# Products of the output projections in the order 2, 1, 4, 6, 5, 7, 3, rows fetched group by group, and the later modulations in other stages

## The chip, the cores and the metric

The kernel runs on one core of a Trainium2 chip. The metric is the device time of one execution in microseconds (us); lower is better. The core has TensorE (PE, matrix products into PSUM banks), VectorE (DVE), ScalarE (ACT) and GpSimd (POOL), and issues transfers (DMAs) from the queues of SyncE (SP) and POOL. Each engine takes its instructions in the order in which they stand in its program.

## The reference, cut to what matters

One layer over 1024 latent tokens and 256 context tokens of width 1024, all in float32. `ml` and `mc` hold nine modulation vectors each, from `silu(c) @ w_mod + b_mod`.

```python
x  = x  + 0.5*ml[2]*swiglu(modulate(rms_norm(x,  g1), ml[0], ml[1]), ffn1_w_in, ffn1_w_out)
cx = cx + 0.5*mc[2]*swiglu(modulate(rms_norm(cx, g1), mc[0], mc[1]), ffn1_w_in, ffn1_w_out)
# mixers on modulate(rms_norm(x, g2), ml[3], ml[4]): gated convolution and attention
x  = x + ml[5]*merge(...)
x  = x + 0.5*ml[8]*swiglu(modulate(rms_norm(x, g3), ml[6], ml[7]), ffn2_w_in, ffn2_w_out)
out = rms_norm(x, final_g)
# swiglu(h, w_in, w_out): a, b = split(h @ w_in); (silu(a)*b) @ w_out, with an inner width of 2816
```

## The kernel before, in words

Activations lie transposed: 128 channels on the partitions, tokens in two chunks C0 and C1 of 512. A float32 product is made of three products of halves: ACT casts an operand to its high part (`rh`, `wh`, ...), DVE subtracts that for the low part (`rl`, `wl`, ...), and PE multiplies high by high, high by low, low by high. Every instruction goes through one helper, so that all rows of the profile name line 88.

The stages follow each other: first modulations and norm; FFN1-in (to about 720 us), 22 columns of the inner width, j = 0 to 21 (L1094); FFN1-out (735 to 956); eight mixers with their weights from `w_in` (956 to 1350, L1191); projections, attention and merge (to about 2100); FFN2-in (to about 2508); FFN2-out with the final norm.

Each FFN-out is `row_products` (L773). It multiplies a 2 x 2 block matrix of weights, A11 to A22, with the 2 x 2 blocks B11 to B22 of the hidden rows in seven products in place of eight (a Winograd scheme). Product i runs over 11 rows of 128, taken in six groups k = 0, 2, 4, 6, 8, 10 (the last has one row), with 12 matmuls a row: 132 matmuls. Products 1, 6 and 7 add up in one set of four PSUM banks, `chain` (names `pt`, `pt`, `po`, `ps`); the others take four of five `ps` banks. At a product's end its banks are added to `x` by DVE (`add`, out of `to`, L859), and only then may a product that uses those banks go on. The order of products stands in L864. `operands` (L815) gives the two operands of a row: the left one from weights (`raw`, or `ws`, where A-sums are made by accumulating DMAs of POOL's queue), the right one from the row tiles (`hid`), which DVE turns into sums in place after their use. The row tiles are written by FFN1-in to DRAM (`hd`) and fetched by `Rows.fetch` (L766), all at once, quadrant after quadrant. In FFN2-out product 3 is made in two halves of 256 tokens: all its split operands are kept (`kept`), so that the second half goes output by output, beside the final norm of the chunks that are done (`final`, L1594).

`after1(i, k)` and `after3(i, k)` (L1144, L1642) are called behind each group and put work in between: loads and stores of the residual `x`, squares for the next norm (`square`), steps of the mixers' first norm (`norm0`, L501: sum of squares of C0, its inverse root `rstd_cols`, a broadcast of that by PE, eight multiplications, splits into the operands `r1` and `r2`).

A later modulation (`later_mod`, L262) is a generator: for each half vector eight loads of `w_mod` (`rawm`), each followed by a multiply-add into `macc` on DVE, then a cast `acch` on ACT with its low part, two matmuls, and four small transfers that turn the row into columns (`mcol`, `modl`): 19 steps a half. FFN1-in runs STEPS[j] steps behind column j (L1100, up to 15), mixers i > 1 run 11 each (L1197), and what is left runs behind the mixers (L1216).

The order on each engine is made at build time by a list scheduler with a model of times; it keeps data dependences and the program order of what is marked (`pinned`, and what is issued while `strict` is set).

Of the kernel before, what the change touches and what calls it, by code (L numbers as in the profile page):

```python
# [18 lines left out]
P = 128  # L19
D = 1024  # L20
# [21 lines left out]
STEPS = (0, 6, 6, 6, 7, 7, 8, 8, 8, 15)  # L42
# [7 lines left out]
def tile_dit_layer(  # L50
# [413 lines left out]
    class Winograd:  # L464
# [6 lines left out]
        def __init__(self, xs, gain, mod, m, pairs, plain=False, ahead=3, side_from=None):  # L471
# [10 lines left out]
            self.n_squares = 0  # L482
# [18 lines left out]
        def norm0(self, in_place=False):  # L501

            acc = sum_squares(self.xs, C0)
            yield
            y = rstd_cols([acc], 512, D)
# [10 lines left out]
        def square(self, d):  # L516

            if not self.n_squares:
                self.acc = [ttile("sq_acc")]
            sq = ttile("sq") if self.n_squares else self.acc[0]  # L520
            act.activation(out=sq, in_=self.xs(d, C1), func=AF.Square)
            if self.n_squares == KD - 1:
                self.acc.append(sq)
            elif self.n_squares:
                dve.tensor_add(out=self.acc[0], in0=self.acc[0], in1=sq)
            self.n_squares += 1

        def norm1(self):
            y = rstd_cols(self.acc, 512, D)
# [215 lines left out]
    class Rows:  # L745


        def __init__(self, n, name):

            self.n, self.t = n, {}  # L750
# [15 lines left out]
        def fetch(self, src):  # L766

            for lower, c in ((0, 0), (0, 1), (1, 0), (1, 1)):
                for k, m in self.groups:
                    j = lower * self.n + k  # L770
                    load(self.t[k, lower, c], src[j : j + m, :, c * 512 : (c + 1) * 512].rearrange("a p n -> p a n"))

    def row_products(w, rows, add, after=lambda i, k: None, halves=False):  # L773
# [9 lines left out]

        R, groups = P * rows.n, rows.groups
        sums = {}
# [12 lines left out]

        def minus(t):
            act.activation(out=t, in_=t, func=AF.Copy, scale=-1.0)  # L800
# [13 lines left out]

        def operands(i, k, m):  # L815
# [174 lines left out]
    half1.acc = accs  # L990
# [39 lines left out]
    def all_later_mods():  # L1030
# [5 lines left out]
        for m in range(2, 9):  # L1036
            yield from later_mod(m)

    steps = all_later_mods()


# [68 lines left out]

    gate1 = half_gate("gate1", 2)
# [22 lines left out]
    hs = Rows(NH // 2, "hid")  # L1134
    hs.fetch(hd)
# [570 lines left out]
```

## Time and profile before

| | |
|---|---|
| median of 3 runs | 2775.6 us (2775.3 to 2777.56) |
| profiled execution | 2770.1 us |
| its span in the trace | 2768.2 us |
| mean granted clock of PE | 0.981 |
| PE busy | 2668.4 us (96%) |
| DVE busy | 2012.0 us (73%) |
| ACT busy | 1153.5 us (42%) |
| DMA, mean | 128 GB/s |

The profile is of one execution. A group row reads: line, engine, operation, output <- inputs, shape, count | total busy, mean ns | idle time before it and what ended it. A waits row reads: engine and output of the one that waited <- what it waited for: us in all, times, the longest. Times in the timeline are counted from the span's start.

### The profile page before, as it was taken

The numbers are of one execution on the slowest core, as the hardware profiler recorded it, in microseconds if no ns is written. First come the engines' busy times: TensorE is split into PE (matmuls) and PEld (weight loads), VectorE is DVE, ScalarE is ACT, GpSimd is POOL, SyncE is SP. The second block draws the span as 40 slices with busy tenths as digits, with TensorE's granted clock in tenths as the row PEclk, the third lists the DMA queues.
The fourth block names the chain that finished last, engine by engine and source line by source line (L and its number), as shares of the span: only waits on it lengthen the run. The fifth ranks groups of instructions, "written<-read, shape, count | busy, mean of one in ns | idle before, by whom it ended". The sixth has DMA issues, their size and how long they took to land.

```text
span 2768.2 us, 37334 instructions
## 1 busy us (share of the span) xinstructions
PE 2668.4 (96%) x13625; PEld 2248.5 (81%) x13625; DVE 2012.0 (73%) x3356; ACT 1153.5 (42%) x2293; POOL 543.0 (20%) x419
## 2 busy tenths in 40 slices
PE   7898999999799999999999999999999999999989
PEld 4687988888677777788899888887888788888878
DVE  5887688887787789887568676685548776568874
ACT  4524333333244552333344566574226333334542
POOL 2240122221011014333123211100000442330110
PEclk8899999999899999999999999999999999999999
DMA  8265433444965244434312311001444542228641
GB/s 308 92 203 159 137 122 122 135 131 150 369 188 112 92 152 151 157 99 134 107 47 63 117 62 61 24 32 41 150 125 129 168 130 76 85 91 292 147 98 62
DMA packets 355649, 354.37 MB, mean 128 GB/s; under 512 B 27382, under 2 KB 248712, under 8 KB 355464
## 3 DMA queue, kind: packets, MB, share of 16 engines
q1 hardware_dynamic: 346440, 334.68, 36.7%
q0 software_dynamic: 9024, 17.30, 4.0%
q8 instruction: 107, 1.75, 0.3%
q14 instruction: 78, 0.64, 0.1%
HBM read 287.91 MB, written 63.96 MB: 127 GB/s over the span
## 4 chain that ended last, share of the span: by engine, by line
PE 80%; DVE 10%; DMA 4%; issue 3%; ACT 2%; POOL 1%; SPq 1%; DVEq 0%; ACTq 0%; POOLq 0%
PE ps L88 66%; PE po L88 7%; PE pt L88 7%; DMA raw<-in_ffn_w_out_dram 2%; DVE wl L88 1%; DVE r L88 1%; DVE macc L88 1%; DMA rawm<-in_w_mod_dram 1%; DVE nt L88 1%; SPq L88 1%; DVE x L88 0%; DMA mcol<-mrow 0%; DVE hid L88 0%; DVE u L88 0%; DVE wo L88 0%
## 5 line engine op out<-in xcount | busy, mean ns | idle before, releaser
L88 PE MATMUL ps<-r,wl 128*128 128x512 f32 x5280 | 1234.2, 393 | 25.4 <-ACT r L88 9.8
L88 PEld LDWEIGHTS ps<-r,wl 128*128 128x128 f32 x5280 | 992.5, 189 | 242.3 <-ACT r L88 12.4
L88 ACT CAST wl<-s 128x512 fp32r<-128x512 f32 x256 | 158.3, 620 | 361.8 <-PE ps L88 270.6
L88 ACT CAST wl<-raw 128x512 fp32r<-128x512 f32 x278 | 172.0, 620 | 283.7 <-PE ps L88 173.5
L88 POOL TENSOR_TENSOR s<-raw 128x512 f32<-128x512 f32 x64 | 97.3, 1521 | 976.3 <-DMA raw<-in_ffn_w_in_dram 553.5
L88 DVE TENSOR_TENSOR wl<-raw,wl 128x512 fp32r<-128x512 f32 x276 | 196.6, 713 | 85.5 <-ACT wl L88 84.2
L88 DVE TENSOR_TENSOR wl<-s,wl 128x512 fp32r<-128x512 f32 x256 | 223.9, 876 | 13.4 <-ACT wl L88 11.7
L88 POOL TENSOR_TENSOR s<-raw,s 128x512 f32<-128x512 f32 x64 | 101.0, 1579 | 404.7 <-DVE wl L88 404.7
L88 DVE SCALAR_TENSOR_TENSOR macc<-rawm,silu_c,macc 128x512 f32<-128x512 f32 x168 | 146.6, 891 | 16.7 <-DMA rawm<-in_w_mod_dram 15.7
L88 PE MATMUL ps<-wh,r 128*128 128x256 f32 x768 | 141.6, 285 | 0.0
L88 DVE TENSOR_TENSOR u<-u,ps 128x512 f32<-128x512 f32 x168 | 114.4, 681 | 34.9 <-PE ps L88 33.3
L88 DVE TENSOR_TENSOR pts<-pt,pts 128x512 fp32r<-128x512 f32 x160 | 108.7, 687 | 42.1 <-ACT pts L88 41.0
L88 ACT CAST rh<-hid 128x512 fp32r<-128x512 f32 x132 | 80.7, 620 | 135.7 <-PE ps L88 103.5
L88 DVE TENSOR_REDUCE m<-ps 128x1 f32<-128x512 f32 (+1 forms) x192 | 110.9, 596 | 28.7 <-PE ps L88 27.7
L88 PE MATMUL ps<-rh,wl 128*128 128x512 f32 x360 | 126.1, 393 | 3.5 <-DVE x L88 3.5
L88 ACT CAST pts<-pt 128x512 fp32r<-128x512 f32 x160 | 93.0, 592 | 86.6 <-PE pt L88 84.9
L88 PEld LDWEIGHTS ps<-wh,r 128*128 128x128 f32 x768 | 120.6, 192 | 0.0
L88 DVE TENSOR_TENSOR rl<-hid,rh 128x512 fp32r<-128x512 f32 x132 | 89.9, 687 | 31.1 <-PE ps L88 29.6
L88 PE MATMUL po<-pts,vh 128*128 128x512 f32 x256 | 110.3, 437 | 1.5 <-ACT pts L88 1.5
L88 PE MATMUL ps<-wl,r 128*128 128x256 f32 x384 | 108.8, 283 | 0.0
L88 ACT CAST wh<-raw 128x512 fp32r<-128x512 f32 (+1 forms) x84 | 67.1, 803 | 95.2 <-PE ps L88 80.2
L88 PE MATMUL ps<-kl,qs 128*128 128x512 f32 x384 | 106.0, 397 | 0.4 <-ACT pc L88 0.4
(280 smaller groups left out, 5098.6 us busy)
## 6 DMA issues: line engine op xcount, KB each, us to landing
raw<-in_ffn_w_in_dram SPq DMA_DIRECT2D x117, 512.0 KB, 4.5
raw<-in_ffn_w_out_dram SPq DMA_DIRECT2D x72, 512.0 KB, 5.7
rawm<-in_w_mod_dram SPq DMA_DIRECT2D x128, 256.0 KB, 4.3
raw<-in_w_in_dram SPq DMA_DIRECT2D x61, 512.0 KB, 3.7
hid<-hd SPq DMA_DIRECT2D x40, 512.0 KB, 9.4
ws<-in_ffn_w_out_dram POOLq DMA_DIRECT2D x30, 512.0 KB, 6.5
hd<-c SPq DMA_DIRECT2D x38, 256.0 KB, 2.0
hd<-u SPq DMA_DIRECT2D x38, 256.0 KB
```

What stands on the lines that cost most here:

```text
L88: inst = getattr(self.engine, name)(*args, **kw)
```

## The change

Products of both FFN-outs come in the order 2, 1, 4, 6, 5, 7, 3. Hidden rows are fetched in pieces, at the start the first two groups of B21, the rest from within products 2 and 1. Sums of rows and weights are made in another way (`sums`), in program order on their engines; s1 = A12 + A22 and s2 = A11 - s1 get buffers of their own. C0's squares for the mixers' norm are made as its rows are done, and the steps of that norm come at other places of products 7 and 3. FFN1-in runs only modulations up to 5; mods 6, 7 and 8 go into mixers i > 1 (13 steps each) and into FFN2-in (3 a column); `gate3` follows FFN2-in. The steps of the final norm come at other groups, and the last chunk's transposes ahead of its inverse root. Cut to its core:

```diff
-STEPS = (0, 6, 6, 6, 7, 7, 8, 8, 8, 15)
+STEPS = (0, 6, 6, 6, 7, 7, 8, 8, 8, 12)
...
-            yield
-            y = rstd_cols([acc], 512, D)
+            if C0 not in self.accs:
+                self.accs[C0] = [sum_squares(self.xs, C0)]
+                yield
+            y = rstd_cols(self.accs[C0], 512, D)
...
+        def square(self, d, ch=C1):
+
+            accs, n = self.accs.setdefault(ch, []), self.n_squares.get(ch, 0)
+            sq = ttile("sq" if n else "sq_acc")
+            act.activation(out=sq, in_=self.xs(d, ch), func=AF.Square)
+            if n in (0, KD - 1):
+                accs.append(sq)
+            else:
+                dve.tensor_add(out=accs[0], in0=accs[0], in1=sq)
+            self.n_squares[ch] = n + 1
 
         def norm1(self):
...
+        def fetch(self, lower, c, to):
+
+            for k, m in self.groups[:to]:
+                if (k, lower, c) not in self.fetched:
+                    self.fetched.add((k, lower, c))
                     j = lower * self.n + k
-                    load(self.t[k, lower, c], src[j : j + m, :, c * 512 : (c + 1) * 512].rearrange("a p n -> p a n"))
+                    load(
+                        self.t[k, lower, c],
+                        self.src[j : j + m, :, c * 512 : (c + 1) * 512].rearrange("a p n -> p a n"),
+                    )
 
     def row_products(w, rows, add, after=lambda i, k: None, halves=False):
...
+        def fetches(i, g):
+
+            if i == 2:
+                rows.fetch(1, 0, g + 3)
+                rows.fetch(1, 1, g + 1)
+                rows.fetch(0, 0, g - 2)
+            elif i == 1:
+                rows.fetch(0, 0, g + 5)
+                rows.fetch(0, 1, g + 2)
+
+        def sums(i, g):
+
+            n = len(groups)
+            if i == 2 and g >= 2 or i == 1 and g < 2:
+                k, _ = groups[g - 2 if i == 2 else n - 2 + g]
+                _, _, b21, b22 = blocks(k)
+                dve.tensor_sub(out=b21, in0=b21, in1=b22)
+            if i == 1 and g or i == 4 and g == 0:
+                k, _ = groups[g - 1 if i == 1 else n - 1]
+                b11, b12, b21, _ = blocks(k)
+                dve.tensor_sub(out=b11, in0=b12, in1=b11)
+                dve.tensor_add(out=b21, in0=b21, in1=b11)
+            if i == 1 and g >= 3 or i == 4 and g < n - 3:
+                k, m = groups[g - 3 if i == 1 else n - 3 + g]
+                s1[k] = atile("ws", (P, 2, 512))[:, :m]
+                load(s1[k], block(k, m, 0, 1))
+                plus(s1[k], k, m, 1, 1)
+            k, m = groups[g]
+            b11, b12, _, b22 = blocks(k)
+            if i == 4:
+                dve.tensor_sub(out=b11, in0=b11, in1=b22)
+                s2[k] = atile("ws", (P, 2, 512))[:, :m]
+                act.activation(out=s2[k], in_=s1[k], func=AF.Copy, scale=-1.0)
+                plus(s2[k], k, m, 0, 0)
+            elif i == 6:
+                dve.tensor_add(out=b11, in0=b11, in1=b22)
+                plus(s2[k], k, m, 1, 0)
+            elif i == 5:
+                dve.tensor_sub(out=b12, in0=b22, in1=b12)
+
         def operands(i, k, m):
 
-            b11, b12, b21, b22 = (rows.t[k, v, c] for v in range(2) for c in range(2))
+            b11, b12, b21, b22 = blocks(k)
             if i in (1, 2, 4):
                 left = part_of_w(k, m, i != 1, i == 4)
             elif i == 7:
                 left, a21 = part_of_w(k, m, 0, 0), part_of_w(k, m, 0, 1)
                 dve.tensor_sub(out=left, in0=left, in1=a21)
             else:
-                left = sums[k]
+                left = (s1 if i == 5 else s2)[k]
             right = {1: b11, 2: b21, 4: b21, 5: b11, 6: b11, 7: b12, 3: b22}[i]
             for e in range(m):
...
                 yield parts(left[:, e], where[0]), parts(right[:, e], where[1])
-            if i == 1:
-                dve.tensor_sub(out=b11, in0=b12, in1=b11)
-            elif i == 2:
-                dve.tensor_sub(out=b21, in0=b21, in1=b22)
-                dve.tensor_add(out=b21, in0=b21, in1=b11)
-            elif i == 4:
-                sums[k] = atile("ws", (P, 2, 512))[:, :m]
-                load(sums[k], block(k, m, 0, 1))
-                plus(sums[k], k, m, 1, 1)
-            elif i == 5:
-                minus(sums[k])
-                plus(sums[k], k, m, 0, 0)
-                dve.tensor_sub(out=b11, in0=b11, in1=b22)
-            elif i == 6:
-                plus(sums[k], k, m, 1, 0)
-                dve.tensor_sub(out=b12, in0=b22, in1=b12)
-
         def step(i, ps, j, l, r, ds=range(4), a=0, n=512):
 
...
-        for i in (1, 2, 4, 5, 6, 7) + (() if halves else (3,)):
+        for i in (2, 1, 4, 6, 5, 7) + (() if halves else (3,)):
             ps = chain if i in (1, 6, 7) else [ps_s() for _ in range(4)]
-            for k, m in groups:
+            for g, (k, m) in enumerate(groups):
                 for e, lr in enumerate(operands(i, k, m)):
+                    if e == 0:
+                        fetches(i, g)
                     step(i, ps, k + e, *lr)
+                strict[0] = True
+                sums(i, g)
+                strict[0] = False
                 after(i, k)
...
-        for m in range(2, 9):
+        for m in range(2, 6):
             yield from later_mod(m)
 
-    steps = all_later_mods()
+    steps, late_steps = all_later_mods(), (step for m in (6, 7, 8) for step in later_mod(m))
...
+    run(steps)
...
-    hs = Rows(NH // 2, "hid")
-    hs.fetch(hd)
+    hs = Rows(hd, NH // 2, "hid")
+    hs.fetch(1, 0, 2)
...
-    residual = {(1, 4): (C0, 0), (2, 2): (C0, 4), (2, 8): (C1, 0), (4, 4): (C1, 4)}
+    residual = {(2, 4): (C0, 0), (1, 6): (C0, 4), (4, 8): (C1, 0), (6, 4): (C1, 4)}
...
     def after1(i, k):
         def done(ds, ch):
             for d in ds:
                 sp.dma_start(out=xd[d, :, ch[1] : ch[1] + 512], in_=xs(d, ch))
-                if ch == C1:
-                    mix.square(d)
+                mix.square(d, ch)
 
         if (i, k) in residual:
             ch, d0 = residual[i, k]
             for d in range(d0, d0 + 4):
                 sp.dma_start(out=xs(d, ch), in_=xd[d, :, ch[1] : ch[1] + 512])
-        if (i, k) == (7, 0):
+        if (i, k) == (5, 0):
             gain2.update(norm_gain("gain2", 3, "g2"))
             mix.gain = gain2["l"]
         if k == NH // 2:
-            if i == 2:
+            if i == 1:
                 done(range(4), C0)
             elif i == 7:
                 done(range(4, KD), C0)
+                run(norms2, 1)
                 done(range(4, KD), C1)
             elif i == 3:
                 done(range(4), C1)
-        if i == 3 and k in (0, 2, 4, 6):
+        if i == 3 and k in (0, 4):
...
-            run(steps, 11)
+            run(late_steps, 13)
         for ch, bg, gc in mixed():
...
-    gate3 = half_gate("gate3", 8)
...
+        def turn(j, half):
+            pt = (ps_o if half and not early else ps_s)()
+            for i in range(4):
+                transpose(pt[:, i * P : (i + 1) * P], yk[half * 4 + i][:, j * P : (j + 1) * P], pinned=early)
+            return pt
+
+        if early:
+            turned = {(j, half): turn(j, half) for half in (1, 0) for j in range(n // P)}
         rstd = rstd_cols(sqs, n, D)
...
-    finals = [final(ch) for ch in last_chunks]
+    seconds_first = (4, 5, 6, 7, 0, 1, 2, 3)
+    finals = [
+        final(ch, *by) for ch, by in zip(last_chunks, ((range(KD),), (seconds_first,), (seconds_first, True)))
+    ]
 
     fast.start(fast.norm1())
     for j in range(NH):
+        if j > 1:
+            run(late_steps, 3)
         u, c = fast.next_first()
         v, b = fast.second(u)
         spill(c, b, j, C0)
         spill(*fast.third(u, v), j, C1)
-    hs = Rows(NH // 2, "hid")
-    hs.fetch(hd)
+    run(late_steps)
+    gate3 = half_gate("gate3", 8)
+    hs = Rows(hd, NH // 2, "hid")
+    hs.fetch(1, 0, 2)
 
...
     def after3(i, k):
 
-        if i == 8 and k == 8:
-            run(finals[0], 4)
+        if i == 5 and k in (2, 4, 6, 8):
+            run(finals[0], 1)
+        if i == 8 and k in (2, 4, 6, 8):
+            run(finals[0], 1)
+        if (i, k) == (8, NH // 2):
+            run(finals[1], 4)
         if i == 9:
-            run(finals[0], 1)
-            if k >= 2:
+            if k in (0, 3, 5, 7, 9):
+                run(finals[0], 1)
+            if k in (1, 2, 3, 4, 6, 8, 10):
                 run(finals[1], 1)
-            if k in (9, 10):
-                run(finals[2], 2)
+            if k in (6, 7, 8, 10):
+                run(finals[2], 1)
 
```

ACT at the end of FFN1-in and the start of FFN1-out. `hidc` is the context's hidden column, `raw` and `wl`/`wh` are weights, `acch` is the cast of the last modulation, and the first `rh` is the first right operand of FFN1-out. Before:

```order
L88 CAST wl_1210_6931<-raw_1209_6929 128x512
L88 CAST wh_1213_6950<-raw_1209_6929 128x512
L88 CAST acch_1142_6648<-macc0_1133_6623 128x512
L88 CAST rh_1186_6803<-hid_1158_6748 128x512
L88 CAST rh_1189_6822<-hid_1158_6748 128x512
L88 CAST rh_1193_6844<-hid_1162_6752 128x512
```

After:

```order
L88 CAST wl_1157_6719<-raw_1156_6717 128x512
L88 CAST hidc_1075_6298<-sa_1102_6502 128x256
L88 CAST rh_1151_6676<-hid_1121_6641 128x512
L88 CAST rh_1154_6701<-hid_1121_6641 128x512
L88 CAST wl_1164_6762<-raw_1163_6760 128x512
L88 ACTIVATE u_1088_6365<-u_1088_6365 128x512
L88 CAST wh_1153_6698<-raw_1149_6671 128x512
```

The `acch` row no longer stands ahead of the first `rh`, which follows the cast of `hidc` and stands ahead of an activation of FFN1-in's last column (`u`).

ACT where product 4 of FFN1-out begins; `wl`/`wh` and `rh` are the operands' high parts, `x1` are rows of the residual. Before, where it follows product 2 (the last row of which is `rh_1272`):

```order
L88 CAST rh_1264_7237<-hid_1176_6766 128x512
L88 CAST wl_1279_7300<-raw_1278_7298 128x512
L88 CAST wh_1282_7319<-raw_1278_7298 128x512
L88 CAST rh_1272_7268<-hid_1179_6769 128x512
L88 CAST rh_1280_7303<-hid_1160_6750 128x512
L88 CAST wl_1287_7343<-raw_1286_7341 128x512
```

After, where it follows product 1:

```order
L88 CAST wh_1273_7363<-raw_1269_7342 128x512
L88 ACTIVATE sq_acc_1234_7181<-x1_1170_6803 128x512
L88 CAST wl_1270_7344<-raw_1269_7342 128x512
L88 ACTIVATE sq_1235_7184<-x1_1171_6805 128x512
L88 ACTIVATE sq_1236_7188<-x1_1172_6807 128x512
L88 ACTIVATE sq_1237_7192<-x1_1173_6809 128x512
L88 CAST rh_1244_7204<-hid_1121_6641 128x512
L88 CAST rh_1247_7223<-hid_1121_6641 128x512
```

The first `rh` of product 4 now has four squares of `x1` ahead of it, which were made elsewhere before.

DVE around the end of product 3 of FFN1-out. `pt` in the `x1` rows is the broadcast inverse root, `gate1` marks the adds of product 3's banks, `r1` is the first right operand of the mixers. Before:

```order
L88 TENSOR_TENSOR wl_1495_8594<-raw_1493_8589,wl_1495_8594 128x512
L88 SCALAR_TENSOR_TENSOR x1_1266_7255<-ps_1442_8281,gate1_l_6724,x1_1266_7255 128x512
L88 TENSOR_TENSOR wl_1497_8599<-raw_1496_8597,wl_1497_8599 128x512
L88 SCALAR_TENSOR_TENSOR x1_1267_7257<-ps_1443_8282,gate1_l_6724,x1_1267_7257 128x512
L88 TENSOR_TENSOR x1_1205_6921<-x1_1205_6921,pt_1470_8435 128x512
L88 TENSOR_TENSOR x1_1206_6923<-x1_1206_6923,pt_1470_8435 128x512
L88 TENSOR_TENSOR x1_1207_6925<-x1_1207_6925,pt_1470_8435 128x512
L88 TENSOR_TENSOR x1_1208_6927<-x1_1208_6927,pt_1470_8435 128x512
L88 TENSOR_TENSOR x1_1205_6921<-x1_1205_6921,pt_1470_8435 128x512
L88 TENSOR_TENSOR x1_1206_6923<-x1_1206_6923,pt_1470_8435 128x512
```

After:

```order
L88 TENSOR_TENSOR wl_1454_8458<-ws_1293_7460,wl_1454_8458 128x512
L88 TENSOR_TENSOR wh_1455_8461<-hid_1140_6660,wh_1455_8461 128x512
L88 TENSOR_TENSOR x1_1170_6803<-x1_1170_6803,pt_1429_8269 128x512
L88 TENSOR_TENSOR x1_1171_6805<-x1_1171_6805,pt_1429_8269 128x512
L88 TENSOR_TENSOR x1_1172_6807<-x1_1172_6807,pt_1429_8269 128x512
L88 TENSOR_TENSOR x1_1173_6809<-x1_1173_6809,pt_1429_8269 128x512
L88 TENSOR_TENSOR x1_1170_6803<-x1_1170_6803,pt_1429_8269 128x512
L88 TENSOR_TENSOR x1_1171_6805<-x1_1171_6805,pt_1429_8269 128x512
L88 TENSOR_TENSOR x1_1172_6807<-x1_1172_6807,pt_1429_8269 128x512
L88 TENSOR_TENSOR x1_1173_6809<-x1_1173_6809,pt_1429_8269 128x512
L88 TENSOR_TENSOR wl_1461_8497<-raw_1460_8495,wl_1461_8497 128x512
L88 TENSOR_TENSOR r1_1430_8276<-x1_1170_6803,r1_1430_8276 128x512
```

The multiplications by the broadcast stood between the adds of product 3; now they stand ahead of all four of them.

More of the change, by code (lines that the diff above doesn't have):

```diff
@@ L514, in norm0 @@
                 yield
[L516 to L526, printed above, removed]
+        def square(self, d, ch=C1):
[7 more added lines that the diff above has]
+            self.n_squares[ch] = n + 1
         def norm1(self):
-            y = rstd_cols(self.acc, 512, D)
+            y = rstd_cols(self.accs[C1], 512, D)
             yield
@@ L764, in tile @@
             return self.t[k - k % 2, j // self.n, c][:, k % 2]
-        def fetch(self, src):
-            for lower, c in ((0, 0), (0, 1), (1, 0), (1, 1)):
-                for k, m in self.groups:
+        def fetch(self, lower, c, to):
+            for k, m in self.groups[:to]:
+                if (k, lower, c) not in self.fetched:
+                    self.fetched.add((k, lower, c))
                     j = lower * self.n + k
-                    load(self.t[k, lower, c], src[j : j + m, :, c * 512 : (c + 1) * 512].rearrange("a p n -> p a n"))
+                    load(
+                        self.t[k, lower, c],
+                        self.src[j : j + m, :, c * 512 : (c + 1) * 512].rearrange("a p n -> p a n"),
+                    )
     def row_products(w, rows, add, after=lambda i, k: None, halves=False):
         R, groups = P * rows.n, rows.groups
-        sums = {}
+        s1, s2 = {}, {}
         def block(k, m, lower, right):
@@ L1214, in tile_dit_layer @@
                 gate(gad, i, ch, g1)
-    run(steps)
     for k in range(4):
@@ L1593, in tile_dit_layer, with final @@
     )
-    def final(ch):
+    def final(ch, order, early=False):
         s, o, n = ch
-        sqs, yk = [], {}
-        for k in (4, 5, 6, 7, 0, 1, 2, 3):
+        sqs, yk, turned = [], {}, {}
+        for i, k in enumerate(order):
             sq = ttile("sq", n)
             act.activation(out=sq, in_=xs(k, ch), func=AF.Square)
-            if k % 2 and (k > 4 or n == 512):
+            if i % 2 and (i < 4 or n == 512):
                 dve.tensor_add(out=sq, in0=sq, in1=sqs.pop())
             sqs.append(sq)
-            if k % 2 == 0:
+            if i % 2 == 0:
                 y2 = atile("yf", (P, 2, 512))
@@ L1613, in final @@
             for half in range(2):
-                pt = (ps_o if half else ps_s)()
-                for i in range(4):
-                    transpose(pt[:, i * P : (i + 1) * P], yk[half * 4 + i][:, j * P : (j + 1) * P])
+                pt = turned.get((j, half)) or turn(j, half)
                 oh = ot[:, half * 512 : (half + 1) * 512]
```

13 lines of the change are left out of this document (6 added, 7 removed).

## The prediction

> **What bounds the kernel now.** I read the page, the waits of TensorE (PE) by stage, the windows, and the timeline at the two longest waits.
>
> ```profile
> span 2768.2 us, 37334 instructions
> PE 2668.4 (96%) x13625; PEld 2248.5 (81%) x13625; DVE 2012.0 (73%) x3356; ACT 1153.5 (42%) x2293; POOL 543.0 (20%) x419
> ```
>
> PE is busy 96% of the span, and the change leaves its products as they are; 2768.2 − 2668.4 leaves 99.8 us of idle PE, plus what a lowered clock adds. So I count waits of PE that go and come. First those from the end of FFN1-in into the mixers (700 to 1075 us), then FFN2-out to the end (2508 on), then one of FFN1-in (135 to 719). The columns are the total in us, the count, and the longest.
>
> ```profile
> PE pt L88 <- ACT rh L88: 15.9, 1, 15.9
> PE ps L88 <- DVE r L88: 3.8, 2, 3.3
> PE ps L88 <- ACT r L88: 3.7, 2, 3.4
> PE ps L88 <- DVE x L88: 2.6, 1, 2.6
> PE pt L88 <- DVE x L88: 2.2, 1, 2.2
> ```
> ```profile
> PE pt L88 <- DVE x L88: 4.3, 1, 4.3
> PE pt L88 <- DVE rl L88: 2.6, 2, 1.9
> PE po L88 <- ACT ot L88: 1.6, 1, 1.6
> PE ps L88 <- DVE x L88: 0.9, 1, 0.9
> ```
> ```profile
> PE ps L88 <- ACT u L88: 3.8, 2, 2.6
> ```
>
> The largest, by its timeline:
>
> ```profile
> 714.82 4.84 PE L88 MATMUL ps<-hidc,wo 128*128 128x256 f32 x39
> 721.57 0.86 SPq L88 DMA_DIRECT2D hid<-hd  x2
> 722.48 4.67 SPq L88 DMA_DIRECT2D rawm<-in_w_mod_dram  x7
> 728.87 5.48 DVE L88 SCALAR_TENSOR_TENSOR macc<-rawm,silu_c,macc 128x512 f32<-128x512 f32 x7 [5.18 <-DMA rawm<-in_w_mod_dram]
> 734.38 0.62 ACT L88 CAST acch<-macc 128x512 fp32r<-128x512 f32 x1 [11.50 <-DVE macc L88]
> 734.91 1.66 ACT L88 CAST rh<-hid 128x512 fp32r<-128x512 f32 x3
> ```
>
> PE ends FFN1-in at 719.66. ACT and DVE work in order, and ahead of the first `rh` stands the cast `acch` of the last modulation, whose seven weight loads were issued only at 722.48. The rows themselves were asked for at 721.57.
>
> **The change part by part.** These windows (us, then busy time of PE, PEld, DVE, ACT, POOL, then granted clock, DMA share, GB/s) bound the rest:
>
> ```profile
> 735.00:766.00 31.00, 30.43 (x124) 24.97 (x124) 26.97 (x38) 10.25 (x19) 2.59 (x2) 0.91 1.07 376
> 766.00:801.00 35.00, 32.45 (x142) 26.22 (x141) 33.71 (x48) 17.51 (x32) 4.59 (x4) 1.00 0.76 203
> 801.00:831.00 30.00, 29.99 (x125) 24.69 (x126) 18.93 (x28) 12.26 (x21) 2.44 (x2) 0.94 0.52 149
> 895.00:925.00 30.00, 30.00 (x133) 24.82 (x133) 17.61 (x28) 9.50 (x17) 0.00 (x0) 1.00 0.30 94
> 1130.00:1350.00 220.00, 220.00 (x972) 181.45 (x971) 176.26 (x259) 73.59 (x125) 72.77 (x48) 1.00 0.37 116
> 2160.00:2508.00 348.00, 347.77 (x1528) 287.88 (x1528) 226.97 (x312) 111.37 (x183) 115.78 (x81) 1.00 0.33 106
> 2540.00:2571.00 31.00, 31.00 (x138) 25.67 (x138) 30.89 (x41) 13.02 (x23) 3.69 (x3) 1.00 0.90 283
> 2675.00:2700.00 25.00, 20.69 (x89) 17.05 (x88) 18.33 (x27) 9.66 (x18) 0.00 (x0) 0.86 0.33 105
> ```
>
> *(a) FFN1-in, 12 steps a column for 15.* The waits on `u` (3.8) come where DVE stands at modulation loads with column work behind. Fewer steps remove some: between 0 and −3.8, I take −2.
>
> *(b) FFN1-in to FFN1-out.* No modulation is left there. `rh` now follows the context's cast, and its first two groups of rows are asked for while the last column runs. −15.9 goes. The clock in the window behind it was 0.91: (1 − 0.91) × 31 = 2.8 us lost, −2.8. Late next is the fetch: I take +1, between 0 and +6 (R2). Sum −17.7.
>
> The Trainium skill ("TensorE: Matmul & The Clock Gate", Part 1) says that PE falls to half clock after an idle window of about 3.4 us and needs as long of work to rise: by that 1.7 us, not 2.8. By the same rule a wait of 2.6 us need not lower the clock; here the 2.6 us wait at 801 left a window at 0.94, while the 2.2 us one at 895 left 1.00, so the rule holds only in part.
>
> *(c) FFN1-out, order 2, 1, 4, 6, 5, 7, 3.* Chain banks and plain ones alternate, so the waits on `x` between products 2 and 4 (2.6) and 6 and 7 (2.2) go, with the clock of the first, (1 − 0.94) × 30 = 1.8: −6.6. New: ACT's first cast for product 4 stands behind four squares, the last of which waits for the add of product 1's last bank. With these rows
>
> ```profile
> L88 DVE TENSOR_TENSOR hid<-hid,hid 128x1024 f32<-128x1024 f32 x25 | 30.5, 1221 | 0.3
> L88 DVE SCALAR_TENSOR_TENSOR x<-ps,gate_l,x 128x512 f32<-128x512 f32 x22 | 15.6, 745 | 2.3 <-PE ps L88 2.3
> L88 ACT CAST rh<-hid 128x512 fp32r<-128x512 f32 x66 | 40.6, 620 | 86.0 <-PE ps L88 57.2 <-issue 23.4 <-DVE hid L88 2.1
> L88 ACT ACTIVATE sq<-x 128x512 f32<-128x512 f32 x11 | 6.4, 623 | 2.1 <-DVE x L88 2.1
> ```
>
> it is 0.745 + 0.623 + 0.620 = 2.0 us, +2 (0 to +4, with a lowered clock). Sum −4.6.
>
> *(d) Product 3 to the mixers.* The broadcast of the first norm stood late:
>
> ```profile
> 954.63 0.60 PE L88 MATMUL pt<-ident,rs_y 128*128 128x128 f32 x4
> 954.98 1.41 PE L88 MATMUL ps<-wh,wl 128*128 128x512 f32 x5
> 959.80 0.79 PE L88 MATMUL ps<-r,wl 128*128 128x512 f32 x1 [3.41 <-ACT r L88]
> 963.89 8.54 PE L88 MATMUL ps<-r,wl 128*128 128x512 f32 x25 [3.30 <-DVE r L88]
> 982.18 21.13 PE L88 MATMUL ps<-r,wl 128*128 128x512 f32 x92
> ```
>
> Product 3 ended at 956.39, 1.8 us after the broadcast began; then came eight multiplications and the splits. Behind the waits 25 matmuls took 8.54 us, 0.342 each against 21.13 / 92 = 0.230: 2.8 us of clock. So 3.4 + 3.3 + 2.8 = 9.5 goes. Now the squares come as rows of `x` finish, and the broadcast stands three rows (some 8 us) ahead of the product's end, before its last adds. But these four adds (3.0 us) and weight splits still stand among the low parts of `r1` on DVE. I take +2.5 (+1 to +6). Sum −7.
>
> *(e) FFN2-out.* The waits on `x` (4.3, 0.9) and `rl` (2.6) go, −7.8. The window of the 4.3 had the clock at 0.86, 3.5 us, part of it within the wait: I take −2. New: four prepared rows of product 3 are there for PE while eight adds (8 × 0.745 = 6.0 us) run, but their splits follow these; +1.5 (0 to +4.5). Sum −8.3.
>
> *(f) The sums of rows.* DVE makes six 128x1024 operations a pair of rows, before five: five full pairs and a half one, 5 × 1.22 + 0.7 = 6.8 us in each FFN-out, 13.6 in all. Cover is DVE's idle time, 0.1 to 12 us of some 31 in the windows above. In products 1 and 4, where they fall, DVE has about as much work as time; in FFN1 the context's adds stand there too. +3 (0 to +13.6). The row loads on SP and the accumulating loads on POOL's queue are as many as before; only their places move.
>
> *(g) The later modulations.* Mods 6 and 7 go into the mixers, mod 8 into FFN2-in. One mod is 16 loads and 16 operations on DVE, in order, so a late load holds column work up. From FFN1-in (two rows), the mixers, and the whole:
>
> ```profile
> DVE macc L88 <- DMA rawm<-in_w_mod_dram: 15.4, 19, 2.2
> L88 DVE SCALAR_TENSOR_TENSOR macc<-rawm,silu_c,macc 128x512 f32<-128x512 f32 x126 | 105.6, 862 | 9.4 <-DMA rawm<-in_w_mod_dram 8.9
> L88 DVE SCALAR_TENSOR_TENSOR macc<-rawm,silu_c,macc 128x512 f32<-128x512 f32 x21 | 21.7, 1033 | 1.8 <-DMA rawm<-in_w_mod_dram 1.6
> PE ps L88 <- DVE wl L88: 4.3, 5, 3.0
> ```
>
> The mixers had 24 such loads (21 here, and three that begin a sum) and get 32; 8 × 1.03 = 8 us more on a DVE that stands idle 44 of 220 us: 0 (−1 to +3, by the 3.0). FFN2-in gets 16, at 0.86 14 us, with 121 of 348 idle: +1.5 (0 to +5).
>
> *(h) The end.* The last chunk's transposes stand ahead of its norm, so the last output needs no bank back:
>
> ```profile
> 2762.72 0.66 PE L88 MATMUL po<-ident,yf 128*128 128x128 f32 x4 [1.63 <-ACT ot L88]
> ```
>
> What stands behind the first ACT output is 0.66 of transposes and what surrounds it; −1 (0 to −1.6).
>
> **Sum.** −2 − 17.7 − 4.6 − 7 − 8.3 + 3 + 0 + 1.5 − 1 = −36.1. The profiled execution took 2770.1 (span 2768.2 and 1.9 around it), 5.5 under the median 2775.6; against its own time the sum gives 2734, carried to the median 2739.5. For small waits like the 0.9 on `x` that an order not yet run may have, I add 1.5: 2741.
>
> **Rivals.**
> *R1, DVE becomes the bound of products 1 and 4.* For: 33.71 busy of 35 and 30.89 of 31 in two windows before, with sums added. Against: products 6, 5, 7 and 3 have over 10 us free each. All 13.6 show, and not 3: 2741 + 10.6 = 2752.
>
> *R2, the rows come late, so that the 15.9 us wait is only replaced.* The 22 pieces of hidden rows are 11.5 MB; at 376 GB/s 31 us, as long as one product, with residual and context loads between. For: DMA at 1.07 in that window. Against: product 2 needs only the lower half of them, 15 us of transfer, spread over its own 31. If PE waits for half a product's rows, 15 us go back: 2756. The Trainium skill ("DMA: Bandwidth & Descriptors", Where 436 GB/s comes from) puts the ceiling at 435 GB/s and an HBM core's share near 358, by which these transfers would take 26 to 32 us, an estimate; the 376 here lies between.
>
> *R3, slower: DVE waits at the moved loads.* The 24 loads that are new to the mixers and FFN2-in have column work right behind them. To turn −35 into +6 they must hold PE up 41 us, 1.7 each; the longest wait of DVE for one was 2.2, though only 19 of over 126 waited, 0.8 on average. At 2.0 each it is 2741 + 48 = 2789. Mixers at 220.00 of 220 busy speak against it.
>
> *R4, it doesn't do what it says: the waits go back to the same engines at other places,* as PE's release is inferred. Then nothing over 0.2% moves: 2774.
>
> **How the numbers follow.** Forecast 0.62, R1 0.17, R2 0.13, R3 0.04, R4 0.04. The forecast's own terms reach from 2732 (f at 0, the new waits of b, d and e at their low ends, a at its gain of 3.8) to 2750 (c, d and g at their high ends). R1 and R2 take the upper end to 2760, leaving out R3, R4 and the tails. 0.2% is 5.6 us, about what a measurement can tell from no change. Faster 0.92, same 0.04, slower 0.04.
>
> **What would show it.** The waits on `rh` at the start of FFN1-out, on `x` before products 4 and 7, and the two on `r` should be gone or under 3 us, and one of about 2 us on `rh` should stand before product 4. Behind product 3 the clock should stay near 1. I am wrong if FFN1-out lasts much over seven times 30 us, if PE waits there for DVE inside product 1 or 4 (R1) or for rows (R2), or if waits on `macc`'s neighbours appear in FFN2-in (R3).

## The result

The kernel after takes 2733.2 us (median of 4 runs, 2731.5 to 2734.96), the kernel before 2775.8 beside it (2775.3 to 2777.56): a ratio of 0.9845, 95% interval 0.9828 to 0.9863. That is 42.6 us less; 2741 was predicted, 2731 to 2760 the range. Part of it lies outside the sum: the profiled execution of before was 5.7 us under this median, that of after (2732.7) only 0.5. Span against span the change is 2768.2 − 2730.9 = 37.3, and the sum was 36.1. The prediction carried its sum to the median by adding the 5.5 us by which before's profiled execution was fast; after has no such offset, and that is most of the 8 us between 2741 and 2733.

The page after, the two rows that answer to those of before:

```profile
span 2730.9 us, 37417 instructions
PE 2658.3 (97%) x13633; PEld 2243.9 (82%) x13633; DVE 2015.1 (74%) x3367; ACT 1153.2 (42%) x2293; POOL 548.8 (20%) x419
```

PE is idle 72.6 us, 99.8 before, and its busy time fell by 10 with the same products: matmuls slowed by a lowered clock became fewer (mean granted clock 0.987, 0.981 before). The waits of PE from 700 to 1075 us, the stretch for which before had 15.9 on `rh` and 28.4 in all:

```profile
PE ps L88 <- DVE wl L88: 3.2, 1, 3.2
PE ps L88 <- ACT rh L88: 2.8, 1, 2.8
PE ps L88 <- DVE rl L88: 1.1, 1, 1.1
PE pt L88 <- DVE rl L88: 0.9, 1, 0.9
...
```

With two of 0.4 and 0.3 they add up to 8.7. From 2480 us to the end no wait of PE is listed, 9.4 before. The seam to FFN1-out, with the first casts of rows, the last 48 context matmuls and the first matmul:

```profile
705.52 1.14 ACT L88 CAST rh<-hid 128x512 fp32r<-128x512 f32 x2
709.61 5.92 PE L88 MATMUL ps<-hidc,wo 128*128 128x256 f32 x48
715.36 0.40 PE L88 MATMUL ps<-rh,wl 128*128 128x512 f32 x1
```

The casts are done before the context's matmuls begin, and PE goes on without a gap. Windows of after (us, busy PE, PEld, DVE, ACT, POOL, clock, DMA share, GB/s): products 2, 1 and 4 of FFN1-out (a few us off at their ends), product 3 into the mixers, their start, a later mixer, and FFN2-out to 31 us before the end:

```profile
715.00:746.00 31.00, 29.89 (x134) 24.46 (x133) 24.24 (x38) 11.93 (x21) 1.36 (x1) 1.00 1.05 384
746.00:780.00 34.00, 31.13 (x137) 25.11 (x135) 32.45 (x45) 15.49 (x28) 3.67 (x3) 1.00 0.77 208
780.00:811.00 31.00, 30.62 (x127) 24.91 (x128) 20.86 (x30) 15.75 (x26) 5.80 (x5) 0.94 0.94 260
930.00:975.00 45.00, 45.00 (x210) 37.49 (x210) 38.98 (x72) 31.51 (x56) 0.00 (x0) 1.00 0.48 152
975.00:1025.00 50.00, 46.79 (x202) 38.09 (x201) 48.63 (x71) 22.75 (x42) 19.09 (x12) 0.97 0.49 158
1075.00:1110.00 35.00, 31.02 (x131) 24.80 (x130) 28.61 (x44) 8.34 (x16) 11.56 (x8) 0.95 0.52 178
2470.00:2700.00 230.00, 230.00 (x1116) 194.74 (x1116) 185.82 (x284) 105.79 (x190) 22.37 (x19) 1.00 0.59 162
```

Product 3 now runs into the mixers with PE full (45.00 of 45). From 2470 to 2700 us, most of FFN2-out, it is full too (230.00 of 230, clock 1.00). FFN1-out is not: in the window of product 1 PE stands 2.9 of 34 us. Of these 0.4 are the wait on `wl`, and 2.5 belong to the wait of 2.8 on `rh` ahead of product 4, from 777.5 to 780.4. DVE is busy 32.45 there.

### The profile page after: what moved, and what is told of

Its sections match the earlier page's. It is cut to its first block, busy times and chain, and to the rows that moved or that the text cites. A ratio compares the mean times of both kernels' runs of the same rounds, so it can differ in the third digit from the quotient of the medians.

```text
span 2730.9 us, 37417 instructions
## 1 busy us (share of the span) xinstructions
PE 2658.3 (97%) x13633; PEld 2243.9 (82%) x13633; DVE 2015.1 (74%) x3367; ACT 1153.2 (42%) x2293; POOL 548.8 (20%) x419
## 3 DMA queue, kind: packets, MB, share of 16 engines
q8 instruction: 107, 1.75, 0.3%
## 4 chain that ended last, share of the span: by engine, by line
PE 80%; DVE 10%; DMA 4%; issue 3%; ACT 2%; POOL 1%; SPq 0%; DVEq 0%; POOLq 0%; ACTq 0%
PE ps L88 65%; PE po L88 8%; PE pt L88 7%; DVE wl L88 1%; DVE macc L88 1%; DVE r L88 1%; DVE nt L88 1%; DMA raw<-in_ffn_w_out_dram 1%; DVE y L88 1%; DVE u L88 1%; DMA raw<-in_ffn_w_in_dram 1%; DMA rawm<-in_w_mod_dram 0%; SPq L88 0%; DMA ws<-in_ffn_w_out_dram 0%; DVE v L88 0%
## 5 line engine op out<-in xcount | busy, mean ns | idle before, releaser
L88 DVE SCALAR_TENSOR_TENSOR macc<-rawm,silu_c,macc 128x512 f32<-128x512 f32 x168 | 144.2, 878 | 10.7 <-DMA rawm<-in_w_mod_dram 10.0
```

Source lines behind the costliest of these rows:

```text
L88: inst = getattr(self.engine, name)(*args, **kw)
```

## The experiments

Each was timed against the kernel before on the same chip. "After" stands for 2733.2 and the ratio 0.9845.

**The modulations where they were, the rest of the change kept.**

```diff
-STEPS = (0, 6, 6, 6, 7, 7, 8, 8, 8, 12)
+STEPS = (0, 6, 6, 6, 7, 7, 8, 8, 8, 15)
...
-        for m in range(2, 6):
+        for m in range(2, 9):
...
-            run(late_steps, 13)
+            run(steps, 11)
...
-            run(late_steps, 3)
...
```

> The changed kernel with the later modulations where they were before (15 steps a column, mods 2 to 8 in FFN1-in and 11 steps a mixer). Theory: the 16 us ahead of FFN1-out were the last modulation's cast in ACT's order, so a wait of 8 to 16 us on rh comes back with its 3 us of clock, and the 3 us in FFN1-in too: 2745 to 2755. Rival: the rows, fetched early and in pieces, removed that wait: at most 2738, with under 3 us of wait there.

2755.1 us (2752.12 to 2758.86), ratio 0.9934 (0.9919 to 0.9949), at the upper end of what the theory expected. Its waits of PE from 720 to 960 us:

```profile
PE ps L88 <- ACT rh L88: 18.9, 2, 16.1
PE pt L88 <- DVE rl L88: 1.9, 1, 1.9
```

The longest is back at the same place with the same length. Its timeline has the same chain:

```profile
731.29 5.47 DVE L88 SCALAR_TENSOR_TENSOR macc<-rawm,silu_c,macc 128x512 f32<-128x512 f32 x7 [4.85 <-DMA rawm<-in_w_mod_dram]
736.80 0.62 ACT L88 CAST acch<-macc 128x512 fp32r<-128x512 f32 x1 [11.17 <-DVE macc L88]
737.33 1.66 ACT L88 CAST rh<-hid 128x512 fp32r<-128x512 f32 x3
```

Early, piecewise rows don't remove the wait; the rival falls.

**The modulations alone, in the kernel before.** The same lines the other way round, order of products and fetch untouched.

> The kernel before with the modulations alone moved as in the change (old order of products, old fetch of all rows at once). Theory: the wait on rh goes (16 + 3 of clock) and 3 us in FFN1-in: 2752 to 2760. Rival: the rows come too late when they are fetched all at once, so that 8 us or more of wait stay: 2764 to 2772.

2747.07 us (2745.09 to 2750.18), ratio 0.9906 (0.989 to 0.9923), 5 us under the lower end expected. Its span (2744.9) is 23.3 under that of before; the rest of the 27 us is that before's profiled execution was fast. No wait on `rh` is left from 700 to 940 us:

```profile
PE ps L88 <- ACT wl L88: 3.1, 1, 3.1
PE pt L88 <- DVE x L88: 2.9, 1, 2.9
PE ps L88 <- ACT r L88: 2.1, 1, 2.1
...
```

So the moved modulations take the wait away by themselves, even with all rows fetched at once in the old order. The ratios of the two experiments give −18 us for everything else and −26 for the modulations; together −44, against −43 for the whole change. Each has an interval of some 4 us to both sides, and within these they add (the spans give −17.9, −23.3 and −37.3).

**The norm at its old place.**

```diff
-                mix.square(d, ch)
+                if ch == C1:
+                    mix.square(d)
...
-                run(norms2, 1)
                 done(range(4, KD), C1)
...
-        if i == 3 and k in (0, 4):
+        if i == 3 and k in (0, 2, 4, 6):
```

> The changed kernel with the squares of C0 and the steps of the mixers' first norm where they were before (all squares inside the norm's first step, steps behind groups 0, 2, 4 and 6 of product 3). Theory: the placement removed the waits at the start of the mixers, so 5 to 9 us come back: 2738 to 2742. Rival: the new order and sums freed DVE there, and the placement does nothing: 2732 to 2735.

2735.68 us (2733.15 to 2739.61), ratio 0.9864 (0.985 to 0.9879). The median leaves both open. The trace does not; PE's waits from 930 to 1010 us, where after has 3.2 on `wl` alone:

```profile
PE ps L88 <- DVE r L88: 4.9, 1, 4.9
PE ps L88 <- ACT r L88: 2.4, 2, 2.1
PE ps L88 <- DVE wl L88: 1.8, 1, 1.8
```

The placement removes the two waits at the seam: the mixers, from the end of product 3 to the first matmul on the context's `h2ch`, last 406.1 us here and 398.8 in after. Its own price is behind product 1, where these squares otherwise don't stand: the wait of 2.8 on `rh` is missing here, though one of 2.8 on `rl` comes in FFN1-out. Net it is 4.6 us in the spans and 2.5 in the medians, with overlapping intervals, so that a net gain is not shown by the times.

**The four squares later.**

```diff
-                mix.square(d, ch)
+                if (i, ch) != (1, C0):
+                    mix.square(d, ch)
...
+        if (i, k) == (4, 4):
+            for d in range(4):
+                mix.square(d, C0)
```

> The changed kernel with the four squares behind product 1 moved into product 4 (behind its group 4). Theory: the 2.8 us wait on rh ahead of product 4 is those squares in ACT's order; it falls under 1 us and its clock loss with it: 2728 to 2731. Rival: DVE's adds and sums hold product 4 anyway, the wait is only put down to another: 2732 to 2735.

2732.29 us (2731.09 to 2733.35), ratio 0.9851 (0.9836 to 0.9866). Ahead of product 4 PE no longer waits, so the squares were that wait. But the time is the same: from 700 to 930 us stands now

```profile
PE pt L88 <- DVE rl L88: 4.1, 2, 3.8
PE pt L88 <- ACT rh L88: 2.3, 1, 2.3
...
```

in product 6 in place of product 4. The `rh` there has its own reason, in ACT's rows:

```profile
805.07 0.63 ACT L88 ACTIVATE ws<-ws 128x512 f32<-128x512 f32 x1 [10.56 <-DMA ws<-in_ffn_w_out_dram]
805.60 0.60 ACT L88 CAST wh<-ws 128x512 fp32r<-128x512 f32 x1
806.11 0.61 ACT L88 CAST rh<-hid 128x512 fp32r<-128x512 f32 x1
```

ACT stands at the last weight sum, whose accumulating transfer is late, and the first row of product 6 is behind it. In after the same row stands at 808.76, later still, and PE, which comes to product 6 only at 812.27, doesn't feel it. The mechanism was right, and the gain was taken by the next wait.

**All rows at once.** In both FFN-outs:

```diff
-    hs.fetch(1, 0, 2)
+    for lower, c in ((1, 0), (1, 1), (0, 0), (0, 1)):
+        hs.fetch(lower, c, NH)
```

> The changed kernel with all hidden rows fetched at once at the start of FFN1-out and of FFN2-out, in the change's order of quadrants (B21, B22, B11, B12). Theory: the transfers have room, and group by group is worth little: 2732 to 2738. Rival (R2 of the prediction): 22 pieces ahead of weights and residual on SP's queue hold up products 2 and 1 of both: 2742 to 2755.

2753.44 us (2752.34 to 2758.7), ratio 0.9927 (0.9913 to 0.9942). My theory falls and the rival holds: piece by piece is worth 20 us in this order. From 700 to 960 us:

```profile
PE ps L88 <- ACT wl L88: 11.4, 1, 11.4
...
```

What waits 11.4 us is a weight cast: the weight loads of product 2 stand in SP's queue behind the pieces. Three of them were issued, first in the experiment and then in after, at

```profile
736.56 1.71 SPq L88 DMA_DIRECT2D raw<-in_ffn_w_out_dram  x3
```

```profile
716.61 2.81 SPq L88 DMA_DIRECT2D raw<-in_ffn_w_out_dram  x3
```

That is 20 us later. R2 of the prediction took this collision for a wait for rows; it is one for the weights queued behind them. FFN2-out loses too: 7.3 us of waits from 2480 to 2700, where after has none.

**More sums on DVE.** An operation that changes nothing behind each group of products 1 and 4:

```diff
+            if i in (1, 4):
+                dve.tensor_tensor(out=b12, in0=b12, in1=b12, op=ALU.max)
```

> The changed kernel with one more 128x1024 DVE operation behind each group of products 1 and 4 (the maximum of a row tile with itself, which changes nothing): 2 x (10 x 1.22 + 2 x 0.69) = 27 us of DVE work in all. Theory: in products 1 and 4 DVE has about as much work as time, so that half or more of it shows: 2746 to 2760. Rival: there is cover left, the sums cost nothing: 2732 to 2738.

2747.21 us (2744.11 to 2748.42), ratio 0.99 (0.9885 to 0.9914): 14 of the 27 us show. In FFN2-out, without a wait in after, stands

```profile
PE ps L88 <- ACT rh L88: 5.9, 1, 5.9
```

and FFN1-out has one of the same length ahead of product 4, 2.8 in after. So products 1 and 4 have little cover left on DVE: R1's mechanism is real, and the sums that the change adds stay below where it shows in FFN2-out.

**Mods 6 and 7 out of the mixers, into the merges.**

```diff
-        if i > 1:
-            run(late_steps, 13)
...
                 run(merge(j, ch))
+                run(late_steps, 6)
```

> The changed kernel with the mods 6 and 7 taken out of the mixers and run in the merge stage, 6 steps behind each merge. Theory: the mixers' waits of 4.1 and 1.0 us with their clock, some 6 us, are the multiply-adds in DVE's order; they go, and the merges, where DVE is less busy, hide them: 2726 to 2730. Rival: these waits come from the norm's and the columns' own work, or come back in the merges: 2732 to 2737.

2728.47 us (2726.28 to 2732.06), ratio 0.9835 (0.982 to 0.985), as the theory expected, though the interval overlaps that of after. In after the mixers from 930 to 1350 us had

```profile
PE ps L88 <- ACT wl L88: 4.2, 2, 4.0
PE ps L88 <- DVE wl L88: 4.1, 2, 3.2
```

and now, from 960 on, only the first of DVE's `wl` is left (and two under 0.5):

```profile
PE ps L88 <- DVE wl L88: 2.8, 1, 2.8
...
```

The 4.0, in after, was six multiply-adds in a row on DVE. ACT stood at the cast `acch` behind them, as at the seam of before; then came column adds on DVE, an activation on ACT and the weight cast:

```profile
1083.14 5.61 DVE L88 SCALAR_TENSOR_TENSOR macc<-rawm,silu_c,macc 128x512 f32<-128x512 f32 x6 [0.84 <-DMA rawm<-in_w_mod_dram]
1088.78 0.62 ACT L88 CAST acch<-macc 128x512 fp32r<-128x512 f32 x1 [9.38 <-DVE macc L88]
1091.90 0.63 ACT L88 ACTIVATE b<-b 128x512 f32<-128x512 f32 x1 [2.50 <-DVE b L88]
1092.44 0.60 ACT L88 CAST wl<-s 128x512 fp32r<-128x512 f32 x1
1093.09 3.18 PE L88 MATMUL ps<-r,wl 128*128 128x512 f32 x7 [3.98 <-ACT wl L88]
```

The mixers last 389.5 us after 398.8, and 389.5 and 390.0 in the two kernels below that have the same move. The merges take the steps without a new wait of note, but what follows the mixers is 4 to 8 us longer in the three (1400.1 to 1404.3 after 1396.5), so that 4 to 8 of the 9 us go back.

**Products 5 and 6 in their old order.**

```diff
-        for i in (2, 1, 4, 6, 5, 7) + (() if halves else (3,)):
+        for i in (2, 1, 4, 5, 6, 7) + (() if halves else (3,)):
...
             if i == 4:
-                dve.tensor_sub(out=b11, in0=b11, in1=b22)
...
             elif i == 6:
-                dve.tensor_add(out=b11, in0=b11, in1=b22)
...
             elif i == 5:
...
+                dve.tensor_sub(out=b11, in0=b11, in1=b22)
...
```

> The changed kernel with products 5 and 6 in their old order (2, 1, 4, 5, 6, 7, 3), the sums of rows fitted to that (B11 less B22 is made behind product 5, and not back again, so five operations a pair of rows in place of six), the residual loads one product earlier. Two changes of bank come back in each FFN-out, 4 to 5 on the plain banks and 6 to 7 on the chain. Theory: each costs a wait on x of 1 to 4 us with some clock, 6 to 12 in all: 2739 to 2745. Rival: DVE's sums cost as much as those waits, so that the order is worth nothing: 2730 to 2735.

2762.12 us (2756.75 to 2764.78), ratio 0.9952 (0.9935 to 0.9969): 29 us, far more than expected. From 700 to 960 us:

```profile
PE ps L88 <- DVE x L88: 9.5, 1, 9.5
PE pt L88 <- DVE x L88: 2.9, 1, 2.9
...
```

In FFN2-out the same two waits are 6.2 and 2.8, with two of 1.1 and 1.0 more: 23.5 us on `x` in all, most of the 29. Why a wait for banks is so dear here, DVE's rows say, the first being a weight split of product 5, the second the add that frees the first bank:

```profile
807.32 0.69 DVE L88 TENSOR_TENSOR wh<-ws,wh 128x512 fp32r<-128x512 f32 x1 [6.10 <-ACT wh L88]
817.82 0.74 DVE L88 SCALAR_TENSOR_TENSOR x<-ps,gate_l,x 128x512 f32<-128x512 f32 x1
```

DVE stood 6.1 us at product 5's weights (ACT waited 10.7 us in all for transfers of weight sums between 790 and 822 us), then worked off the last sums of product 4, and the adds stand among these. In after it is no better at the same place, where product 6 comes next:

```profile
809.93 0.69 DVE L88 TENSOR_TENSOR wh<-ws,wh 128x512 fp32r<-128x512 f32 x1 [8.59 <-ACT wh L88]
818.46 0.74 DVE L88 SCALAR_TENSOR_TENSOR x<-ps,gate_l,x 128x512 f32<-128x512 f32 x1
```

DVE stands even longer and the first add is later, but PE has been in product 6 since 812.27, in the other banks. So DVE is behind in both kernels, and the changed order pays because PE can go on meanwhile. That holds with the change's sums: in the kernel before the two changes of bank cost 2.6 and 2.2.

**One sum on POOL.**

```diff
-                dve.tensor_sub(out=b21, in0=b21, in1=b22)
+                pool.tensor_sub(out=b21, in0=b21, in1=b22)
```

> The changed kernel with one of the six sums of a row pair (B21 less B22, in products 2 and 1) on POOL in place of DVE: some 6.8 us less DVE work in each FFN-out. Theory: DVE's load bounds products 1 and 4 of FFN1-out, so 2 to 5 of the 8 us that PE loses there go: 2728 to 2731. Rival: those waits hang on ACT's order (the squares) and on PSUM adds, or POOL is too slow for its reader: 2732 to 2738.

2733.53 us (2732.01 to 2736.53), ratio 0.9855 (0.984 to 0.987): no gain. From 700 to 940 us the waits on `rl` shrink from 2.0 to 0.3, but the 2.8 on `rh` stays; some 2 us less there don't show in the median, which lies in the rival's range. By the trace both are half right: the small waits were DVE's load, the largest was ACT's order.

**The last transposes behind the norm's sums.**

```diff
+        rstd = rstd_cols(sqs, n, D)
         if early:
             turned = {(j, half): turn(j, half) for half in (1, 0) for j in range(n // P)}
-        rstd = rstd_cols(sqs, n, D)
```

> The changed kernel with the last chunk's transposes issued behind the matmuls of its norm in place of ahead of them. Theory: pinned ahead, these 16 transposes (1.9 us of PE) delay the norm's column sums by about 1.0 us, and behind them they lie beside the inverse root on DVE: the last 13 us shorten by 1 to 1.5 us, 2731.5 to 2732.5, to be read in the trace more than in the median. Rival: the end is bound by the last output's transfer: no change.

2731.49 us (2730.77 to 2735.62), ratio 0.9847 (0.9833 to 0.9861), not to be told from after. The end can be read in the trace. The last add to `x` and the last column sums, in after (span 2730.9):

```profile
2718.01 0.48 DVE L88 SCALAR_TENSOR_TENSOR x<-ps,gate_l,x 128x256 f32<-128x256 f32 x1 [0.68 <-PE ps L88]
2720.00 2.74 PE L88 MATMUL pt<-ones,sq 128*128 128x1 f32 x24
```

and in the experiment (span 2733.8):

```profile
2722.65 0.48 DVE L88 SCALAR_TENSOR_TENSOR x<-ps,gate_l,x 128x256 f32<-128x256 f32 x1 [0.68 <-PE ps L88]
2723.95 1.62 PE L88 MATMUL pt<-ones,sq 128*128 128x1 f32 x14
2725.43 1.94 PE L88 MATMUL ps<-ident,yf 128*128 128x128 f32 x16
```

From the add to the end it is 12.9 us in after, 11.15 here. In before the add stood at 2756.35 of 2768.2, 11.85. So the change made its end about 1 us longer: the transposes, pinned ahead, held up the sums. Put behind them, they give 1.75 us back in the trace.

**Together.** The two that stand by themselves:

> The two that stand by themselves together: mods 6 and 7 in the merge stage, and the last transposes behind the norm's sums. Expected 2727 if they add (4.7 measured for the first, 1 to 1.5 for the second); 2728.5 if the second is nothing.

2725.26 us (2720.86 to 2729.97), ratio 0.9824 (0.9807 to 0.9841): the best of all, by about 0.2% under after, with overlapping intervals. And with the sum on POOL:

> All three: mods 6 and 7 in the merge stage, the last transposes behind the norm's sums, and B21 less B22 on POOL. If DVE's load is the bound in FFN1-out: 2723 to 2726. If not: as the one without the POOL sums, about 2727, or slower by what POOL delays.

2728.4 us (2724.86 to 2733.83), ratio 0.9837 (0.9819 to 0.9854). POOL adds nothing that can be told, and FFN2-out gets a wait on `rl` of 2.8, which after hasn't.

## Why the prediction was right, point by point

- *(a) FFN1-in*, −2 taken: the waits on `u` (3.8) are gone, some waits on the context's activation are longer; all waits of PE from 135 us to the seam are 14.6 after 17.1, −2.5. The stage ends 4.1 us earlier; the other 1.6 stand in no wait.
- *(b) The seam*, −17.7 taken: −15.9 and the clock from 0.91 to 1.00 in the window behind it (2.8), with a new wait on `rl` of 1.1 in product 2: −17.6. Both experiments on the modulations name the cause. That the fetch is no wait here holds in the changed order only for rows in pieces; in the old order it holds for all at once as well.
- *(c) FFN1-out's order*, −4.6 taken, and this is the step that failed. The bank waits (2.6 and 2.2) went, but 2.8 on `rh`, 0.9 on `rl` and 0.4 on `wl` came, and behind the 2.8 the clock is 0.94 (780 to 811), as it was behind the 2.6 before: −0.7. I had priced the squares at 2.0 without a loss of clock (only the bound of +4 had one), and left out that ACT and DVE have hardly room for the work that is moved between these products. That the order takes the bank waits away is shown by the old one, where they are 9.5 and 2.9; but in FFN1-out it gains no time, as the table below shows.
- *(d) Product 3 to the mixers*, −7 taken: the 3.4, the 3.3 and the clock (9.5) went entirely, and not 2.5 but 3.2 came back, not at the seam (935.6) but 55 us on (990.58, on `wl`), with a clock of 0.97 over 50 us, 1.5: −4.8, or −5.6 with the small waits on `r` of before in that stretch (0.8). DVE makes the split for that `wl` at 989.85; ACT's cast for it was done at 985.83, and 4 us of other work, most of it on the mixers' right operands (`r`, `nt`), stand between. The wait is there without the modulations too (2.8), so these are not its cause.
- *(e) FFN2-out*, −8.3 taken: all 7.8 and the clock went (2 as taken, 3.5 in that window at most) and nothing came: −9.8 to −11.3.
- *(f) The sums*, +3 taken: no wait in FFN2-out, and in FFN1-out they are part of (c). They are real work at the edge: 27 us more cost 14.
- *(g) Modulations*, +1.5 taken: FFN2-in lists no wait of PE from 2140 to 2470. In the mixers 4.0 came and 3.0 went, both with a clock of 0.95 in the 35 us around them: +1, within the bounds. Against the experiment with the old modulations the mixers are 3.2 longer (398.8 after 395.6) and what follows them 1.4 (1396.5 after 1395.1), one execution each; with the mods in the merges the mixers are 9.3 shorter.
- *(h) The end*, −1 taken: +1.0, since I looked at the last bank and not at what the transposes now stand in front of.

Measured, these add up to −33 to −36 of the 37.3 between the spans. The same change by the length of each stretch (us), beside the experiment with the modulations alone; the prediction's (f) is put half to each FFN-out:

| stretch, to the end of | before | modulations alone | after | predicted | measured |
|---|---|---|---|---|---|
| FFN1-in | 719.7 | 715.0 | 715.5 | −2 | −4.1 |
| FFN1-out with its seam | 236.7 | 219.5 | 220.1 | −20.8 | −16.6 |
| the mixers | 405.1 | 404.7 | 398.8 | −7 | −6.3 |
| the kernel | 1406.8 | 1405.7 | 1396.5 | −6.3 | −10.3 |

Up to the end of FFN1-out the modulations alone do all that the change does: together, the order, the pieces and the sums bring no time there, within the 2 to 3 us by which this stretch differs among kernels that don't differ in it (218.6 to 223.0). What these bring comes later, in the mixers (where the old place of the norm gives 406.1 us) and in FFN2-out. FFN1-out fell 4 us short and the rest of the kernel gave 4 more, so that the total came out nearer than its parts: that is luck.

The signs named ahead came: no wait on `rh` at the seam, none on `x`, the two on `r` gone, 2.8 on `rh` ahead of product 4, a clock of 1.00 behind product 3. R3 did not come: where loads had to be waited for in FFN2-in (2 waits of DVE, 2.6 us), PE had work. The mechanism of R1 and the transfers of R2 both show in experiments, with more sums and with all rows at once, and not in the change as it stands. One sum of the prediction is off: with (c), (d) and (g) at their high ends, the mixers' +3 included, the terms reach 2753 and not 2750.

What stays open: why the profiled execution of before was 5.7 under its median, and why a wait of 2.8 to 3.8 us stays in FFN1-out whichever of its causes is taken away.

## What to carry to other kernels

When an engine takes its work in order, look behind a seam for what stands in front of the first instruction of the next stage; here that was a cast of the last modulation, moving the modulations to later stages was worth 26 of 43 us, and the earlier fetch did not replace it. Alternating two sets of banks between products hides the adds of one under the matmuls of the next: where DVE had stood for 6 and 9 us, PE waited 9.5 us for banks in the old order and for none in the new one. In FFN1-out, whose helpers have little room, both experiments that took away the wait of 2.8 us on `rh` got another, of 2.8 and 3.8, in the same stage; so price such a stage by the helpers' load and not by the wait.

## What the runs showed of the hardware that was not expected

PE's clock drops without a wait. In the experiment on the end, nine 128x256 matmuls behind 24 one-column sums took

```profile
2708.35 2.74 PE L88 MATMUL pt<-ones,sq 128*128 128x1 f32 x24
2710.95 2.18 PE L88 MATMUL ps<-kept,kept 128*128 128x256 f32 x9
```

and in after, at the same place of the program,

```profile
2705.30 2.74 PE L88 MATMUL pt<-ones,sq 128*128 128x1 f32 x24
2707.89 1.32 PE L88 MATMUL ps<-kept,kept 128*128 128x256 f32 x9
```

PE was busy throughout in both, and the granted clock was 0.75 from 2708 to 2714 us in the experiment and 1.00 from 2705 to 2711 in after. Of the twelve kernels that have these two groups of matmuls, five took 1.32 or 1.33 for the nine in their profiled execution and seven 1.84 to 2.27; six of the seven had no wait of PE in the 40 us before. So a stretch of such sums can cost the clock, and need not. The whole differs between executions of one kernel: the best kernel's four runs had spans of 2728.2 at a mean clock of 0.986, 2724.0 and 2723.0 at 0.988, and 2719.0 at 0.990. The Trainium skill ("TensorE: Matmul & The Clock Gate", Part 1) says that the gate's window runs freely and that the clock follows how busy PE has been. That the same rows lose clock in one execution and not in another agrees with the first; how little a one-column matmul counts as busy no row shows by itself. Span times clock is 2690 to 2692 in all four of the best kernel's runs, so that the 9 us between them go with the clock; how much of that these sums cost is not shown.
